# Fused hybrid-attention layer: q turned as unsplit pairs of heads, the windowed branch's output halves added on GpSimd, its row sums copied by VectorE

## The chip, the cores and the metric

The kernel runs on one core of one Trainium2 chip. A core has a matrix engine (TensorE, PE in the profile), VectorE (DVE), ScalarE (ACT), GpSimd (POOL) and a DMA-issuing engine (SyncE, SP). Each has its own instruction queue and works through it in order; the engines meet through semaphores. The metric is the time of one execution in microseconds, the median of several runs.

## What is computed

One layer of a diffusion backbone over 1024 latent tokens of width 1024 with 256 context tokens, batch 1, in float32. The tokens are modulated and projected; then two attentions run over the same tokens, each with 8 query heads of width 64 and 2 key heads (so four query heads share a key head):

```python
# windowed: |q_pos - k_pos| <= 128 and all 256 context keys, with a sink logit
scores = where(mask, q @ k.T / 8, -inf)
m = maximum(max(scores), sink); e = exp(scores - m)
p = e / (sum(e) + exp(sink - m));  o_a = p @ v
# global: all 1024 + 256 keys, q and k normalised
o_b = softmax(qn @ kn.T / 8) @ v
y = (g_a * (o_a @ w_branch_a) + g_b * (o_b @ w_branch_b)) @ w_out
```

A layer norm, a gated convolutional feed-forward block and a second layer norm follow. The change touches only the two attentions.

## The kernel before, in words

**Split numbers.** Products need more precision than one pass of the matrix engine gives, so a float32 operand is written as a rounded high part (type fp32r) and a remainder. The helper `split` (recorded at L84 and L87) does it in two instructions: a rounding copy and a subtraction.

**Units.** The attentions are cut into 32 units. A unit is one branch (0 windowed, 1 global), one tile `i` of 128 queries (0 to 7) and one key head `g` (0 or 1), with its four query heads; its name is branch_i_g, and in instruction names of the windowed branch this text writes i_g. Units 0 to 15 are windowed and take the stretch from about 330 to 455 us of the span, units 16 to 31 are global and end at about 722 us.

**Steps of a unit.** Each unit goes through these steps:

- `qprep`, two units ahead of its use: the 128x256 piece of q for four heads is split by GpSimd into `qs`, where each head has its 64 high and 64 low columns side by side. Four transposes on PE (L486) turn it, ScalarE copies the 128x512 result to `q1` (L489), with high parts on partitions 0 to 63 and low ones on 64 to 127, and two DMAs on SP's queue (L490, L491) write `q2` with the two halves exchanged. `qk` (L496, L497) multiplies keys with q1 and then q2, which gives all four products of high and low parts.
- `lat`, once for each head `h`: PE makes the scores (with the mask as one more matmul, L528, in the windowed branch), VectorE scales them into the tile `p` and takes the row's extreme (L545), ScalarE takes the exponential and the row sum (L547). In the windowed branch the row has one more column, the sink logit. GpSimd writes it for all four heads at once, ahead of head 0 (L542, `p<-sinkb`). A windowed row is 640 scores wide in the inner tiles, 641 with the sink.
- `norm` and `rows`: VectorE takes reciprocals of the row sums (L563), PE turns them (L567), in the windowed branch ScalarE copies the 4x128 result out of PSUM (L573), and SP writes it to DRAM (`dn`, L576) and reads it back spread over the partitions (`rb`, L578).
- value steps, one for each of 5 key tiles (10 in the global branch): four transposes of `p` on PE (L604), a split into `pth` (ScalarE, L615) and `ptl` (VectorE, L616), and two matmuls into `av` (L627, L628). For key tile 1 of a windowed unit (tiles 2 and 6 of a global one) the split is given to GpSimd: ScalarE copies the turned tile to the buffer `side` (L612), and GpSimd writes `pth` and `ptl` (L84, L87).
- `out_step`: ScalarE copies `av` to `side` (L639), GpSimd moves its lower half to `up` (L640), two adds of 64x256 make the output `ot` (L643), GpSimd multiplies it by `rb` (L646) and splits it into two parts `O` (L84, L87). The two adds run on VectorE for windowed tiles 0 to 5 (and in the very last unit), on GpSimd otherwise.

**What sets the order.** Scores of a unit and value steps of the unit before are interleaved by fixed fractions of a turn. In the windowed and global stages the instruction order on each engine comes out of a scheduler that works from that sequence, so an edit in one step can move others. The tile `p` has two buffers, so scores of the next unit are written while PE still turns the present one. `side` has two slots, used in turn.

Of the kernel before, what the change touches and what calls it, by code (L numbers as in the profile page):

```python
# [7 lines left out]
F32 = mybir.dt.float32  # L8
R32 = mybir.dt.float32r
AF = mybir.ActivationFunctionType  # L10
ALU = mybir.AluOpType
AX = mybir.AxisListType

P = 128
# [4 lines left out]
NT = 8  # L19
HD = 64  # L20
# [49 lines left out]
def layer_kernel(  # L70
# [6 lines left out]
    nc = tc.nc  # L77
    PSUM = bass.MemoryType.PSUM

    def split(src, hi, lo, hi_eng, lo_eng):  # L80
        if hi_eng is nc.scalar:
            nc.scalar.copy(hi, src)  # L82
        elif hi_eng is nc.gpsimd:
            nc.gpsimd.tensor_scalar(out=hi, in0=src, scalar1=1.0, scalar2=0.0, op0=ALU.mult, op1=ALU.add)  # L84
        else:
            hi_eng.tensor_copy(hi, src)
        lo_eng.tensor_tensor(out=lo, in0=src, in1=hi.bitcast(F32), op=ALU.subtract)  # L87
# [11 lines left out]
    ident = ctile([P, P], F32, "ident")  # L99
    identr = ctile([P, P], R32, "identr")  # L100
# [39 lines left out]
    qp = tc.alloc_tile_pool(name="qp", bufs=1, side="right", reuse_waits="tile")  # L140
# [144 lines left out]
    for k in range(KT):  # L285
# [9 lines left out]
        h, w = hT[k], w0[k]  # L295
# [84 lines left out]
    def qtile(br, t):  # L380
        return Q[br, t - t % 2][:, t % 2]
# [84 lines left out]
    class Unit:  # L466
# [11 lines left out]

        def qprep(self, mk=None):
            nm = self.id  # L480
            q3 = qtile(self.br, self.i)[:, self.g * 256:(self.g + 1) * 256].rearrange("p (h d) -> p h d", d=HD)
            qs = qp.tile([P, 4, P], R32, tag="qs", name=f"qs{nm}", bufs=2)
            split(q3, qs[:, :, 0:HD], qs[:, :, HD:P], nc.gpsimd, nc.gpsimd)
            tr = (mk or pt_tile)(f"qtr{nm}", R32)
            for h in range(4):
                nc.tensor.transpose(tr[:, h * P:(h + 1) * P], qs[:, h], identr)  # L486
            q1 = qp.tile([P, 512], R32, tag="q1", name=f"q1{nm}", bufs=2)
            q2 = qp.tile([P, 512], R32, tag="q2", name=f"q2{nm}", bufs=2)
            nc.scalar.copy(q1, tr)  # L489
            nc.sync.dma_start(q2[0:HD].bitcast(F32), q1[HD:P].bitcast(F32))  # L490
            nc.sync.dma_start(q2[HD:P].bitcast(F32), q1[0:HD].bitcast(F32))  # L491
            self.q = q1, q2

        def qk(self, o, h, ks, stop=True):
            hs = slice(h * P, (h + 1) * P)
            nc.tensor.matmul(o, self.q[0][:, hs], ks, start=True, stop=False)  # L496
            nc.tensor.matmul(o, self.q[1][:, hs], ks, start=False, stop=stop)  # L497
# [67 lines left out]
        def rows(self):  # L565
            tr = pt_tile(f"str{self.id}")
            nc.tensor.transpose(tr[0:4, 0:P], self.sm, ident)  # L567
            self.rb = att.tile([P, 2, P], F32, tag="rb", name=f"rb{self.id}", bufs=2)
            row = self.rb[0:4, 0]
            if self.br:  # L570
                nc.vector.reciprocal(row, tr[0:4, 0:P])
            else:
                nc.scalar.copy(row, tr[0:4, 0:P])  # L573
            dn = dpool.tile([4, P], F32, tag=f"dn{self.id}", name=f"dn{self.id}")
            tokens.append(f"dn{self.id}")
            nc.sync.dma_start(dn, row)  # L576
            for a in range(2):
                nc.sync.dma_start(self.rb[a * HD:(a + 1) * HD],  # L578
                                  dn.rearrange("(b a) q -> a b q", a=2)[a].partition_broadcast(HD))
# [15 lines left out]
        def value_steps(self):  # L595
            nm, kt = self.id, self.kt
# [33 lines left out]
            def out_step():  # L630
                av = self.av
                up = att.tile([HD, 512], F32, tag="up", name=f"up{nm}", bufs=1)
                ot = att.tile([P, 2, P], F32, tag="ot", name=f"ot{nm}", bufs=1)
                if last:
                    low = av
                    nc.scalar.copy(up, av[HD:P])
                else:
                    low = side_tile()
                    nc.scalar.copy(low, av)  # L639
                    nc.gpsimd.tensor_scalar(out=up, in0=low[HD:P], scalar1=1.0, scalar2=0.0, op0=ALU.mult, op1=ALU.add)  # L640
                oe = nc.gpsimd if (self.br or self.i >= NT - 2) and not last else nc.vector
                for h in range(2):
                    oe.tensor_tensor(out=ot[h * HD:(h + 1) * HD],  # L643
                                     in0=low[0:HD].rearrange("p (a b q) -> p a b q", b=2, q=P)[:, :, h],
                                     in1=up.rearrange("p (a b q) -> p a b q", b=2, q=P)[:, :, h], op=ALU.add)
                (nc.vector if last else nc.gpsimd).tensor_tensor(out=ot, in0=ot, in1=self.rb, op=ALU.mult)  # L646
                hf = self.i // 4
                qs = slice((self.i % 4) * P, (self.i % 4 + 1) * P)
                split(ot, otile(self.br, hf, 0, self.g)[:, :, qs], otile(self.br, hf, 1, self.g)[:, :, qs],
                      *((nc.scalar, nc.vector) if last else (nc.gpsimd, nc.gpsimd)))  # L650
# [1286 lines left out]
```

## Time and profile before

| | |
|---|---|
| median of 3 runs | 1526.8 us (1524.75, 1526.8, 1527.01) |
| profiled execution | 1523.1 us |
| its span | 1521.3 us |
| mean TensorE clock granted | 0.997 |
| windowed stage, about | 330 to 455 us |
| global stage, about | 455 to 722 us |

The profile gives the busy time of each engine (PEld is PE's weight load, which overlaps its matmuls), the instructions with start and duration, and for an idle time the instruction whose end released it. A timeline row reads: start in us, duration, engine, line, operation, tile written <- tiles read, shape and type, count, and in brackets the idle time ahead of it with its releaser. A group row reads: line, engine, operation, tiles, shape and count, then busy us and mean ns, then idle time. The ends of PE's instructions are modelled.

### The profile page before, as it was taken

The page shows a single profiled execution, that of the slowest core. Times are in us where ns is not written, and L with a number is a line of the kernel's source. Part 1 is how long each engine was busy: PE and PEld are TensorE (multiplying, and loading weights), DVE is VectorE, ACT ScalarE, POOL GpSimd, SP SyncE. Part 2 cuts the span into 40 slices and gives each one's busy share as a digit, 9 for nine tenths or more (in the row PEclk, how much of TensorE's full clock was granted, in tenths as well). Part 3 has the DMA queues.
Part 4 walks back from the last instruction along what each step waited for, and adds up shares of the span by engine and source line. Part 5 has one row for each costly group of instructions (what it writes and reads, how often), then busy time and mean ns, then how long its engine had stood idle before and what let it go on. Part 6 is the DMA issues. An engine that isn't in the chain of part 4 may idle for free.

```text
span 1521.3 us, 22183 instructions
## 1 busy us (share of the span) xinstructions
PE 1503.2 (99%) x7812; PEld 1263.3 (83%) x7812; DVE 1168.3 (77%) x1751; ACT 786.1 (52%) x1303; POOL 751.3 (49%) x727
## 2 busy tenths in 40 slices
PE   8999999999999999999999999999999999999997
PEld 7888888888988888887888998888888888888887
DVE  6667986539988787877865788888888888557884
ACT  5322222439988677667234555444444444435552
POOL 0356532426776677766124346666666773111121
PEclk9999999999999999999999999999999999999998
DMA  9777672322234576653541322333344448996731
GB/s 370 266 242 242 223 252 87 106 82 68 67 108 104 131 172 167 153 121 89 207 160 42 104 77 98 111 111 111 111 111 111 112 111 238 340 271 210 255 105 56
DMA packets 114399, 232.09 MB, mean 153 GB/s; under 512 B 13200, under 2 KB 28048, under 8 KB 114192
## 3 DMA queue, kind: packets, MB, share of 16 engines
q1 hardware_dynamic: 99056, 201.82, 39.8%
q0 software_dynamic: 10400, 20.19, 8.8%
q10 hardware_dynamic: 4832, 8.68, 1.5%
q8 instruction: 61, 1.00, 0.3%
q14 instruction: 50, 0.41, 0.1%
HBM read 179.45 MB, written 65.86 MB: 161 GB/s over the span
## 4 chain that ended last, share of the span: by engine, by line
PE 92%; DVE 3%; ACT 2%; issue 1%; DMA 1%; POOL 1%; SPq 0%; DVEq 0%; ACTq 0%; POOLq 0%
PE ptr L604 5%; PE p L90 4%; PE p L91 4%; PE p L92 4%; PE g L90 4%; PE g L92 4%; PE g L91 4%; PE av L627 4%; PE av L628 3%; PE b L90 3%; PE b L92 3%; PE b L91 3%; PE s L496 3%; PE s L497 3%; PE c L90 2%; PE c L92 2%
## 5 line engine op out<-in xcount | busy, mean ns | idle before, releaser
L616 DVE TENSOR_TENSOR ptl<-ptr,pth 128x512 fp32r<-128x512 f32 x195 | 128.2, 685 | 20.2 <-ACT pth L615 18.0
L547 ACT ACTIVATE p<-p,nm 128x1280 f32<-128x1280 f32 (+2 forms) x128 | 139.8, 1093 | 6.6 <-DVE p L545 5.9
L87 DVE TENSOR_TENSOR ld<-rd,hd 128x1024 fp32r<-128x1024 f32 x77 | 94.8, 1250 | 50.5 <-ACT hd L82 48.3
L615 ACT CAST pth<-ptr 128x512 fp32r<-128x512 f32 x195 | 111.3, 590 | 30.3 <-PE ptr L604 28.7
L82 ACT CAST hd<-rd 128x1024 fp32r<-128x1024 f32 x77 | 79.3, 1048 | 82.2 <-PE p L92 55.7
L604 PEld LDWEIGHTS ptr<-identr,pb 128*128 128x128 f32 x944 | 96.3, 140 | 23.7 <-ACT pb L550 3.0
L604 PE MATMUL ptr<-identr,pb 128*128 128x128 f32 x944 | 107.5, 245 | 1.5 <-ACT pb L550 1.0
L87 POOL TENSOR_TENSOR wlg<-wg,whg 128x512 fp32r<-128x512 f32 x32 | 48.6, 1529 | 121.7 <-ACT whg L82 80.8
L627 PE MATMUL av<-pth,VT 128*128 128x512 f32 x236 | 104.2, 441 | 0.5 <-ACT side L639 0.3
L90 PE MATMUL p<-hd 128*128 128x512 f32 x264 | 103.2, 391 | 0.0
L92 PE MATMUL p<-hd,ld 128*128 128x512 f32 x264 | 102.8, 389 | 0.0
L91 PE MATMUL p<-ld,hd 128*128 128x512 f32 x264 | 102.7, 389 | 0.0
L90 PE MATMUL g<-hh,whg 128*128 128x512 f32 x256 | 99.9, 390 | 0.0
L92 PE MATMUL g<-hh,wlg 128*128 128x512 f32 x256 | 99.7, 389 | 0.0
L91 PE MATMUL g<-hl,whg 128*128 128x512 f32 x256 | 99.6, 389 | 0.0
L628 PE MATMUL av<-ptl,VT 128*128 128x512 f32 x236 | 97.5, 413 | 0.3 <-DVE ptl L616 0.2
L545 DVE TENSOR_SCALAR_CACHE_REDUCE p<-s,cvt,nmc 128x1024 f32<-128x1024 f32 x64 | 84.2, 1317 | 5.2 <-PE s L497 5.2
L496 PE MATMUL s<-KL,q 128*128 128x512 f32 (+2 forms) x192 | 73.6, 384 | 1.3 <-DVE p L545 0.8
L497 PE MATMUL s<-KL,q 128*128 128x512 f32 (+2 forms) x192 | 71.8, 374 | 0.0
L783 ACT ACTIVATE sg<-g,bgc 128x512 f32<-128x512 f32 x32 | 22.0, 686 | 96.2 <-PE g L92 91.4
L82 ACT CAST wS<-s 128x512 fp32r<-128x512 f32 x76 | 45.3, 620 | 48.7 <-POOL s L1236 47.9
L82 ACT CAST wA<-ru 128x512 fp32r<-128x512 f32 x57 | 35.5, 623 | 62.6 <-PE d L92 33.6
(434 smaller groups left out, 4866.9 us busy)
## 6 DMA issues: line engine op xcount, KB each, us to landing
wml<-in_wmodT_dram SPq DMA_DIRECT2D x48, 512.0 KB
ru<-in_w_up_dram SPq DMA_DIRECT2D x38, 512.0 KB
rd<-td SPq DMA_DIRECT2D x55, 256.0 KB
rd<-sd SPq DMA_DIRECT2D x44, 256.0 KB
rd<-in_w_dn_dram SPq DMA_DIRECT2D x33, 256.0 KB
wm<-in_wmodT_dram SPq DMA_DIRECT2D x16, 512.0 KB
wg<-in_w_g_dram SPq DMA_DIRECT2D x32, 256.0 KB
sgd<-sg ACTq DMA_DIRECT2D x32, 256.0 KB
```

Of the source, the lines that this page charges most:

```text
L82: nc.scalar.copy(hi, src)
L87: lo_eng.tensor_tensor(out=lo, in0=src, in1=hi.bitcast(F32), op=ALU.subtract)
L90: nc.tensor.matmul(ps, a[0], b[0], start=start, stop=False, skip_group_check=resumed)
L91: nc.tensor.matmul(ps, a[0], b[1], start=False, stop=False, skip_group_check=resumed)
L92: nc.tensor.matmul(ps, a[1], b[0], start=False, stop=stop, skip_group_check=resumed)
L496: nc.tensor.matmul(o, self.q[0][:, hs], ks, start=True, stop=False)
L497: nc.tensor.matmul(o, self.q[1][:, hs], ks, start=False, stop=stop)
L547: nc.scalar.activation(row, row, AF.Exp, bias=self.nm[:, hs], scale=-1.0, accum_out=self.sm[:, hs])
L604: i = nc.tensor.transpose(tr[:, h * P:(h + 1) * P], self.bits[:, h, n * P:(n + 1) * P], identr)
L616: nc.vector.tensor_tensor(out=lo, in0=tr, in1=hi.bitcast(F32), op=ALU.subtract)
L627: nc.tensor.matmul(self.av, v, hi, start=first, stop=False)
L628: nc.tensor.matmul(self.av, v, lo, start=False, stop=self.left == 0)
```

## The change

Three edits, all in the attention units; the mask stays a matmul.

1. `qprep`: q is no longer split before it is turned. PE makes two float32 transposes, each of a pair of heads (128x128), into a 128x256 PSUM tile. ScalarE writes the rounded part `qx`, VectorE the remainder `qy` (both 128x256). Eight DMAs of 64x256 on SP's queue put each half of `qx` into both halves of q1's partitions and each half of `qy` into both of q2's, so q1 holds high parts twice and q2 low parts twice. `qk` picks the columns of a head accordingly.
2. `rows`: the windowed branch's 4x128 copy goes from ScalarE to VectorE.
3. `out_step`: the two adds run on GpSimd in every unit but the last.

```diff
@@ -478,20 +478,22 @@
 
         def qprep(self, mk=None):
             nm = self.id
-            q3 = qtile(self.br, self.i)[:, self.g * 256:(self.g + 1) * 256].rearrange("p (h d) -> p h d", d=HD)
-            qs = qp.tile([P, 4, P], R32, tag="qs", name=f"qs{nm}", bufs=2)
-            split(q3, qs[:, :, 0:HD], qs[:, :, HD:P], nc.gpsimd, nc.gpsimd)
-            tr = (mk or pt_tile)(f"qtr{nm}", R32)
-            for h in range(4):
-                nc.tensor.transpose(tr[:, h * P:(h + 1) * P], qs[:, h], identr)
-            q1 = qp.tile([P, 512], R32, tag="q1", name=f"q1{nm}", bufs=2)
-            q2 = qp.tile([P, 512], R32, tag="q2", name=f"q2{nm}", bufs=2)
-            nc.scalar.copy(q1, tr)
-            nc.sync.dma_start(q2[0:HD].bitcast(F32), q1[HD:P].bitcast(F32))
-            nc.sync.dma_start(q2[HD:P].bitcast(F32), q1[0:HD].bitcast(F32))
-            self.q = q1, q2
+            q2 = qtile(self.br, self.i)[:, self.g * 256:(self.g + 1) * 256]
+            tr = (mk or pt_tile)(f"qtr{nm}")[:, 0:2 * P]
+            for j in range(2):
+                nc.tensor.transpose(tr[:, j * P:(j + 1) * P], q2[:, j * P:(j + 1) * P], ident)
+            hi, lo = (qp.tile([P, 2 * P], R32, tag=f"q{a}", name=f"q{a}{nm}", bufs=2) for a in "xy")
+            nc.scalar.copy(hi, tr)
+            nc.vector.tensor_tensor(out=lo, in0=tr, in1=hi.bitcast(F32), op=ALU.subtract)
+            self.q = [qp.tile([P, 512], R32, tag=f"q{n}", name=f"q{n}{nm}", bufs=2) for n in (1, 2)]
+            for q, part in zip(self.q, (hi, lo)):
+                for a in range(2):
+                    for b in range(2):
+                        nc.sync.dma_start(q[b * HD:(b + 1) * HD, a * 256:(a + 1) * 256].bitcast(F32),
+                                          part[a * HD:(a + 1) * HD].bitcast(F32))
 
         def qk(self, o, h, ks, stop=True):
+            h = h % 2 * 2 + h // 2
             hs = slice(h * P, (h + 1) * P)
             nc.tensor.matmul(o, self.q[0][:, hs], ks, start=True, stop=False)
             nc.tensor.matmul(o, self.q[1][:, hs], ks, start=False, stop=stop)
@@ -570,7 +572,7 @@
             if self.br:
                 nc.vector.reciprocal(row, tr[0:4, 0:P])
             else:
-                nc.scalar.copy(row, tr[0:4, 0:P])
+                nc.vector.tensor_copy(row, tr[0:4, 0:P])
             dn = dpool.tile([4, P], F32, tag=f"dn{self.id}", name=f"dn{self.id}")
             tokens.append(f"dn{self.id}")
             nc.sync.dma_start(dn, row)
@@ -638,7 +640,7 @@
                     low = side_tile()
                     nc.scalar.copy(low, av)
                     nc.gpsimd.tensor_scalar(out=up, in0=low[HD:P], scalar1=1.0, scalar2=0.0, op0=ALU.mult, op1=ALU.add)
-                oe = nc.gpsimd if (self.br or self.i >= NT - 2) and not last else nc.vector
+                oe = nc.vector if last else nc.gpsimd
                 for h in range(2):
                     oe.tensor_tensor(out=ot[h * HD:(h + 1) * HD],
                                      in0=low[0:HD].rearrange("p (a b q) -> p a b q", b=2, q=P)[:, :, h],
```

Lines after the edit in `qprep` stand two higher than in the kernel before (L542 becomes L544, and so on).

The first place is GpSimd's queue in the middle of the windowed stage. In the names, `p_3_1<-sinkb` is the sink column of unit 3_1, and `pth`, `ptl`, `up`, `ot` carry their unit; the number at the end only tells tiles apart. Before:

```order
L542 TENSOR_SCALAR p_3_1_3822<-sinkb 128x4 [waits PE_49]
L646 TENSOR_TENSOR ot_2_0_3777<-ot_2_0_3777,rb_2_0_3621 128x256 [waits DMAHW6_49,DMAHW5_49,DVE_49]
L84 TENSOR_SCALAR O_3268<-ot_2_0_3777 128x2x128 [waits Pool_49]
L87 TENSOR_TENSOR O_3269<-ot_2_0_3777,O_3268 128x2x128 [waits Pool_49]
L84 TENSOR_SCALAR pth_3_0_1_3848<-side 128x512 [waits Activation_49]
L87 TENSOR_TENSOR ptl_3_0_1_3849<-side,pth_3_0_1_3848 128x512 [waits PE_49,Pool_49]
L84 TENSOR_SCALAR qs_5_1_4164<-Q_4_1588 128x4x64 [waits PE_49]
L640 TENSOR_SCALAR up_2_1_3902<-side 64x512 [waits Activation_49,Pool_49]
L87 TENSOR_TENSOR qs_5_1_4164<-Q_4_1588,qs_5_1_4164 128x4x64 [waits Pool_49]
L542 TENSOR_SCALAR p_4_0_3948<-sinkb 128x4 [waits PE_49]
```

and after:

```order
L544 TENSOR_SCALAR p_3_0_3728<-sinkb 128x4 [waits PE_49]
L84 TENSOR_SCALAR pth_2_1_1_3754<-side 128x512 [waits DVE_49,Activation_49]
L87 TENSOR_TENSOR ptl_2_1_1_3755<-side,pth_2_1_1_3754 128x512 [waits PE_49,Pool_49]
L642 TENSOR_SCALAR up_2_0_3808<-side 64x512 [waits Activation_49,Pool_49]
L645 TENSOR_TENSOR ot_2_0_3809<-side,up_2_0_3808 64x256 [waits Pool_49]
L645 TENSOR_TENSOR ot_2_0_3809<-side,up_2_0_3808 64x256
L648 TENSOR_TENSOR ot_2_0_3809<-ot_2_0_3809,rb_2_0_3649 128x256 [waits DMAHW2_49,DMAHW1_49,Pool_49]
L84 TENSOR_SCALAR O_3284<-ot_2_0_3809 128x2x128 [waits Pool_49]
L87 TENSOR_TENSOR O_3285<-ot_2_0_3809,O_3284 128x2x128 [waits Pool_49]
L544 TENSOR_SCALAR p_3_1_3858<-sinkb 128x4 [waits PE_49]
```

Between two sink columns there stood the product and `O` of one unit, then `pth`, `ptl`, `up` and q's split; the column came ahead of the product. Now the whole output of unit 2_0, its two halves included, stands between `up` and the column of unit 3_1, and the column comes last.

The second place is ScalarE's queue at the same units: the exponentials that wait for GpSimd are head 0 of units 3_0 and 3_1. Before:

```order
L547 ACTIVATE p_3_0_3696,sm_3_0_3695<-p_3_0_3696,nm_3_0_3694 128x641 [waits DVE_49,Pool_49]
L612 COPY side<-ptr_2_1_1_3717 128x512 [waits PE_49]
L573 COPY rb_2_1_3747<-str_2_1_3745 4x128 [waits DMAHW1_49,DMAHW0_49,DMAHW7_49,PE_49,Pool_49]
L615 CAST pth_2_1_2_3768<-ptr_2_1_2_3763 128x512 [waits DVE_49,PE_49]
L547 ACTIVATE p_3_0_3696,sm_3_0_3695<-p_3_0_3696,nm_3_0_3694 128x641 [waits DVE_49]
L639 COPY side<-av_2_0_3682 128x512 [waits PE_49]
L547 ACTIVATE p_3_0_3696,sm_3_0_3695<-p_3_0_3696,nm_3_0_3694 128x641 [waits DVE_49]
```

and after:

```order
L549 ACTIVATE p_3_0_3728,sm_3_0_3727<-p_3_0_3728,nm_3_0_3726 128x641 [waits DVE_49,Pool_49]
L617 CAST pth_2_1_0_3734<-ptr_2_1_0_3729 128x512 [waits PE_49]
L614 COPY side<-ptr_2_1_1_3749 128x512 [waits PE_49]
L617 CAST pth_2_1_2_3800<-ptr_2_1_2_3795 128x512 [waits DVE_49,PE_49]
L641 COPY side<-av_2_0_3714 128x512 [waits PE_49]
L549 ACTIVATE p_3_0_3728,sm_3_0_3727<-p_3_0_3728,nm_3_0_3726 128x641 [waits DVE_49] x3
L486 CAST qx_4_0_3821<-qtr_4_0_3818 128x256 [waits DMAHW6_49,DMAHW3_49,DMAHW7_49,DMAHW2_49,PE_49]
L552 CAST pb_3_0_3793<-onec 128x1 [waits Activation_49]
L617 CAST pth_2_1_3_3840<-ptr_2_1_3_3835 128x512 [waits PE_49]
L617 CAST pth_2_1_4_3852<-ptr_2_1_4_3847 128x512 [waits PE_49]
L549 ACTIVATE p_3_1_3858,sm_3_1_3857<-p_3_1_3858,nm_3_1_3856 128x641 [waits DVE_49,Pool_49]
```

In both, head 0 of a unit stands ahead of the copy `side<-ptr` of the unit before it, for which GpSimd's `pth` waits. The `pth` cast that stood ahead of the exponential now stands between it and that copy, the row copy `rb<-str` is gone, and `qx` has half the width.

The third place is SP's queue there, with `dn` and `rb` of unit 2_0 or 2_1 and the q copies of later units. Before:

```order
L578 DMA rb_2_0_3621<-dn_2_0_3623 64x2x128 [waits DMAHW5_49,DMAHW6_49,DMAHW4_49,Pool_49]
L578 DMA rb_2_0_3621<-dn_2_0_3623 64x2x128
L490 DMA q_3_1_3669<-q_3_1_3668 64x512 [waits Activation_49]
L491 DMA q_3_1_3669<-q_3_1_3668 64x512 [waits DMAHW0_49]
L576 DMA dn_2_1_3749<-rb_2_1_3747 4x128 [waits DMAHW1_49,Activation_49]
L578 DMA rb_2_1_3747<-dn_2_1_3749 64x2x128 [waits DMAHW2_49,DMAHW1_49,Pool_49]
L578 DMA rb_2_1_3747<-dn_2_1_3749 64x2x128 [waits DMAHW3_49]
```

and after:

```order
L580 DMA rb_2_0_3649<-dn_2_0_3651 64x2x128 [waits DMAHW5_49,DMAHW1_49,Pool_49]
L580 DMA rb_2_0_3649<-dn_2_0_3651 64x2x128 [waits DMAHW2_49]
L492 DMA q_3_1_3695<-qx_3_1_3691 64x256 [waits DMAHW3_49]
L492 DMA q_3_1_3695<-qx_3_1_3691 64x256 [waits DMAHW4_49]
L492 DMA q_3_1_3696<-qy_3_1_3692 64x256 [waits DVE_49,PE_49]
L492 DMA q_3_1_3696<-qy_3_1_3692 64x256 [waits DMAHW6_49]
L492 DMA q_3_1_3696<-qy_3_1_3692 64x256 [waits DMAHW7_49]
L492 DMA q_3_1_3696<-qy_3_1_3692 64x256 [waits DMAHW0_49]
L578 DMA dn_2_1_3781<-rb_2_1_3779 4x128 [waits DMAHW1_49,DVE_49]
L492 DMA q_4_0_3825<-qx_4_0_3821 64x256 [waits DMAHW2_49,PE_49,Activation_49]
L580 DMA rb_2_1_3779<-dn_2_1_3781 64x2x128 [waits DMAHW3_49,DMAHW1_49,Pool_49]
L580 DMA rb_2_1_3779<-dn_2_1_3781 64x2x128 [waits DMAHW4_49]
```

Two q copies a unit have become eight, some of them wait for VectorE's `qy`, and they stand in between a unit's `dn` and its `rb`.

## The prediction

> **What bounds the kernel now.** I read the page first, for what is busy, then the busy time by stretch, then the timelines of the windowed stage.
>
> ```profile
> PE 1503.2 (99%) x7812; PEld 1263.3 (83%) x7812; DVE 1168.3 (77%) x1751; ACT 786.1 (52%) x1303; POOL 751.3 (49%) x727
> ```
>
> PE is busy nearly throughout, but its ends are modelled, so the two attention stages need a closer look. By stretch (busy us of PE, PEld, DVE, ACT, POOL; then clock, DMA share, GB/s):
>
> ```profile
> 360.00:440.00 80.00, 79.43 (x567) 70.95 (x566) 73.79 (x157) 73.86 (x175) 62.52 (x94) 1.00 0.29 75
> 470.00:720.00 250.00, 249.10 (x1526) 204.21 (x1524) 200.80 (x387) 179.04 (x313) 173.94 (x218) 1.00 0.60 140
> ```
>
> In the global stage (470 to 720) PE has 0.9 us idle in 250 while DVE, ACT and POOL have 49 to 76 us to spare: only PE counts there. In the windowed stage (360 to 440) PE, DVE and ACT are all above 92%, and POOL has 17.5 us idle. There a queue that waits can lengthen the turn. One turn of POOL's queue, from one unit's pooled part to the next:
>
> ```profile
> 401.61 0.62 POOL L84 TENSOR_SCALAR pth<-side 128x512 fp32r<-128x512 f32 x1 [0.76 <-PE str L567]
> 402.31 1.29 POOL L87 TENSOR_TENSOR ptl<-side,pth 128x512 fp32r<-128x512 f32 x1
> 403.99 0.41 POOL L84 TENSOR_SCALAR qs<-Q 128x256 fp32r<-128x256 f32 x1 [0.38 <-PE qtr L486]
> 404.47 0.62 POOL L640 TENSOR_SCALAR up<-side 64x512 f32<-64x512 f32 x1
> 405.18 0.97 POOL L87 TENSOR_TENSOR qs<-Q,qs 128x256 fp32r<-128x256 f32 x1
> 406.12 0.37 POOL L542 TENSOR_SCALAR p<-sinkb 128x4 f32<-128x4 f32 x1
> 406.51 0.75 POOL L646 TENSOR_TENSOR ot<-ot,rb 128x256 f32<-128x256 f32 x1
> 407.35 0.40 POOL L84 TENSOR_SCALAR O<-ot 128x256 fp32r<-128x256 f32 x1
> 407.84 0.74 POOL L87 TENSOR_TENSOR O<-ot,O 128x256 fp32r<-128x256 f32 x1
> ```
>
> The row to watch is the sink column (L542), 0.37 us. The first exponential of a unit reads that column, so it cannot start before POOL has written it. The same write at other units gives the turn's length:
>
> ```profile
> 361.28 0.20 POOL L542 TENSOR_SCALAR p<-sinkb 128x4 f32<-128x4 f32 x1
> 367.01 0.38 POOL L542 TENSOR_SCALAR p<-sinkb 128x4 f32<-128x4 f32 x1
> 436.91 0.37 POOL L542 TENSOR_SCALAR p<-sinkb 128x4 f32<-128x4 f32 x1
> 447.15 0.21 POOL L542 TENSOR_SCALAR p<-sinkb 128x4 f32<-128x4 f32 x1
> ```
>
> The second and third belong to units 2_1 and 7_0, nine turns apart: (436.91 - 367.01) / 9 = 7.77 us a turn.
>
> **The output halves, and the place of the sink column.** On VectorE a half takes 416 ns alone; on GpSimd, where the global units already do it, 734 ns:
>
> ```profile
> L643 POOL TENSOR_TENSOR ot<-side,up x38: 721/734/742, 442.6 to 713.1; 64x256 f32<-64x256 f32 x38
> L643 DVE TENSOR_TENSOR ot<-side,up x24: 416/590/1486, 349.9 to 436.3; 64x256 f32<-64x256 f32 x24
> 405.13 1.30 DVE L643 TENSOR_TENSOR ot<-side,up 64x256 f32<-64x256 f32 x2 [0.60 <-POOL up L640]
> ```
>
> VectorE loses 1.30 + 0.60 = 1.9 us a turn, its wait for `up` included. The q split leaves POOL (0.41 + 0.97) and two halves come (about 1.5), so POOL's load hardly changes. What changes is the order. In POOL's new queue the sink column of unit n+1 stands behind the pooled `pth` and `ptl` of unit n-1 and the whole output of n-2: `up`, two halves, product with `rb`, both parts of `O`; before, it stood ahead of the last three. On ScalarE the first exponential of unit n stands ahead of the copy `side<-ptr` of n-1, which feeds that `pth`. This closes a ring: sink column, exponential, side copy, the whole POOL chain, next sink column. Its length is one turn at the least.
>
> The POOL part, with a unit of the windowed end where GpSimd already does the halves, and the only steady write that follows an `O`:
>
> ```profile
> 441.88 0.61 POOL L640 TENSOR_SCALAR up<-side 64x512 f32<-64x512 f32 x1 [2.53 <-ACT side L639]
> 442.58 1.53 POOL L643 TENSOR_TENSOR ot<-side,up 64x256 f32<-64x256 f32 x2
> 444.19 0.73 POOL L646 TENSOR_TENSOR ot<-ot,rb 128x256 f32<-128x256 f32 x1
> 360.58 0.73 POOL L87 TENSOR_TENSOR O<-ot,O 128x256 fp32r<-128x256 f32 x1
> ```
>
> From start to start: `pth` 0.70, `ptl` 1.29 (its row), `up` 0.70, two halves 1.61, product 0.84, `O` 0.49, its remainder 0.70 (360.58 to 361.28), sink column 0.20. Sum 6.53 us. The ScalarE part:
>
> ```profile
> 361.51 0.84 ACT L547 ACTIVATE p<-p,nm 128x641 f32<-128x641 f32 x1 [0.46 <-DVE ptl L616]
> 362.35 0.56 ACT L612 COPY side<-ptr 128x512 f32<-128x512 f32 x1
> 406.04 0.59 ACT L615 CAST pth<-ptr 128x512 fp32r<-128x512 f32 x1
> 406.51 0.21 ACT L550 CAST pb<-onec 128x1 fp32r<-128x1 f32 x1
> 400.95 0.58 ACT L612 COPY side<-ptr 128x512 f32<-128x512 f32 x1
> ```
>
> The exponential at 361.51 starts 0.03 after the column's end at 361.48, after 0.46 idle; the profile names VectorE, but the column is what came last, so this wait exists already where `O` stands ahead. Then 0.84 to the next instruction, 0.47 for the `pth` cast that stands between (406.04 to 406.51), 0.58 for the copy and 0.08 until POOL starts (401.53 to 401.61): 2.00 us. The ring is 6.53 + 2.00 = 8.53 us against 7.77. Bounds: bare durations without gaps give about 8.05; a column of 0.37, as in most rows, gives 8.70. I take 8.53, since the gaps are measured. Nine turns: 9 x 0.76 = +6.8 us (2.5 to 8.4).
>
> The Trainium skill, GPSIMD Engine Reference, section "4.1 Engine selection", speaks against this edit: elementwise work with two inputs belongs on VectorE, GpSimd being about twice as slow. The rows give 734 / 416 = 1.76, so the direction agrees and the size is smaller; at twice 416 the ring would be 0.2 us longer and the sum 1.8 us higher (an estimate from that page).
>
> The ramp and the tail of the stage: the turn from 361.28 to 367.01 takes 5.73 us now and would take the ring's 8.53, +2.8, but the write at 361.28 itself stands earlier in the new order, ahead of the product and `O`, which can give it all back: +1.5 (0 to 2.8). The last turn, 436.91 to 447.15, is 10.24 us now; at 8.53 it gives back 1.7: -1.5 (-1.7 to 0).
>
> **The row copy.** ScalarE loses sixteen copies, VectorE gains them.
>
> ```profile
> L573 ACT COPY rb<-str x16: 238/254/256, 344.9 to 456.4; 4x128 f32<-4x128 f32 x16
> ```
>
> On VectorE no such row exists; the nearest is its 128x4 reciprocal, 0.18, below, so 0.2 a turn. VectorE has 1.9 us freed and ScalarE idles inside the ring: nothing on the path (-0.25 to +0.25 a turn if neither cover held, which the ring excludes).
>
> ```profile
> 406.46 0.18 DVE L563 RECIPROCAL sm<-sm 128x4 f32<-128x4 f32 x1
> ```
>
> **The q turn.** On PE four fp32r transposes become two fp32 ones of the same size:
>
> ```profile
> 573.07 0.46 PE L486 MATMUL qtr<-identr,qs 128*128 128x128 f32 x4
> 573.36 0.33 PE L604 MATMUL ptr<-identr,pb 128*128 128x128 f32 x2
> 1483.28 0.42 PE L1758 MATMUL zt<-ident,pr 128*128 128x128 f32 x2
> 1483.54 0.28 PE L1761 MATMUL stl<-onec,pr 128*128 128x1 f32 x2
> ```
>
> Four took 0.29 to the next start, two fp32 ones 0.26: PE is even (at most 0.03 x 32 = -1 us). ScalarE's cast halves, from 0.58 to some 0.35 (between 0.25 and 0.58); VectorE gains a 128x256 subtraction, between the 0.2 of the reciprocal and the 0.69 of `ptl`, say 0.4. Both lie beside PE in the global stage (49 us of VectorE spare for 15 units' 6 us) and inside the ring in the windowed one. With that cover gone they would cost 0.4 x 10 = 4 us. The q DMAs:
>
> ```profile
> 405.36 0.50 SPq L490 DMA_DIRECT2D q<-q  x1
> 405.90 0.60 SPq L491 DMA_DIRECT2D q<-q  x1
> 403.11 1.29 SPq L578 DMA_DIRECT2D rb<-dn  x2
> 401.90 0.26 SPq L576 DMA_DIRECT2D dn<-rb  x1
> ```
>
> Two become eight, 8 x 0.55 = 4.4 us of SP's queue where 1.1 stood; with the 1.29 and 0.26 it holds 5.95 us of a turn of 8.5. Behind the waiting q copies stand `dn` and `rb`, for which POOL's product waits, and the loads of the stage. q is made two units ahead, so I cost this at nothing; the bound is rival C.
>
> The Trainium skill, DMA: Bandwidth & Descriptors, section "Measured (HBM→SBUF, 128 partitions, SWDGE, issued from GpSimd)", says that transfers should be batched and that those under 64 KB are dominated by their descriptors; eight quarter pieces go against that. It bears on rival C; no run here shows transfers of this size on that queue, and the sum goes by the issue rows.
>
> Global stage: 0 (-0.5 to +1), since PE alone counts. Sum: 6.8 + 1.5 - 1.5 + 0 = +6.8 us (0.3 to 12.2). The profiled execution took 1523.1 us and would take 1529.9; it lies 3.7 us under the median of the runs, so on the median of 1526.8 the forecast is **1533.6 us**, by itself 1527 to 1539.
>
> **The rivals.** *A, relief:* if the ring is shorter than I read (the column early enough), the freed VectorE and ScalarE time shortens the turn until PE binds. For it: PE's value matmuls are slower here than over the program,
>
> ```profile
> L627 PE MATMUL av<-pth,VT 128*128 128x512 f32 x51 | 23.4, 460 | 0.3 <-ACT side L639 0.3
> L627 PE MATMUL av<-pth,VT 128*128 128x512 f32 x236 | 104.2, 441 | 0.5 <-ACT side L639 0.3
> ```
>
> so the turn could fall by 441/460 to 7.45: 10 x -0.32 = -3.2, and -1 at the tail, -4.2: 1522.6 us. Against it: the ring's rows. It decides for itself only if the ring is under 7.45. *B, no change:* the ring is there but comes out at about 7.7, hidden by the present turn: 1526 us. It needs POOL's chain 0.8 us shorter than its rows. *C, the q copies bind:* if each of the eight issues or its landing takes about 0.9 us instead of 0.55, SP's queue is full for 8 x 0.9 + 1.55 = 8.75 us a turn, POOL's product waits for `rb` inside the ring, and a turn goes to about 9: ten turns x 0.5 = +5 more, 1539 us.
>
> **How the numbers follow.** Forecast 0.63, A 0.13, B 0.12, C 0.12. The range 1524 to 1540 leaves out about half of A and a third of C. What a measurement can tell from no change is 0.2%, 3.05 us. Faster (under 1523.7): 0.10 of A and 0.01 of B, 0.11. Same: 0.03 of A, 0.09 of B, 0.06 of the forecast's low end, 0.18. Slower: 0.57 of the forecast, C and 0.02 of B, 0.71.
>
> **What would show it.** Right: sink columns 8.3 to 8.7 us apart between units 2_1 and 7_0; ScalarE idle ahead of the first exponential, which starts within 0.1 us of the column's end; POOL's wait ahead of `pth` (0.76 us above) released by the side copy; PE under 95% busy from 360 to 440. The global stage keeps its length within 1 us. Wrong: columns 7.4 to 7.8 us apart (A or B); or POOL's product idle for `rb`, or PE's first score matmul for q (C).

## The result, and the profile after

The changed kernel takes 1535.62 us (median of 6 runs, 1534.33 to 1537.28) against 1525.55 us for the kernel before (6 runs, 1524.66 to 1527.01). The ratio is 1.0065, 95% interval 1.0052 to 1.0078: slower by some 10 us. The prediction was 1533.6 us, or 6.8 us more than before. The profiled execution of the changed kernel took 1537.28 us, with a span of 1535.5 us, and lies 1.7 us above its median; that of before lies 2.5 us under its own. So the two profiles are 14.2 us apart, and what follows shares out those 14.2 us. In the experiments below, one run of the halves alone took 1646.13 us at a granted clock of 0.85 and is left out of its median.

The page's busy times, and the two stretches that the prediction began with:

```profile
PE 1504.7 (98%) x7748; PEld 1261.2 (82%) x7748; DVE 1172.2 (76%) x1775; ACT 777.9 (51%) x1287; POOL 729.0 (47%) x687
```

```profile
360.00:440.00 80.00, 73.58 (x493) 63.11 (x492) 59.61 (x136) 61.90 (x146) 56.10 (x85) 0.98 0.38 90
470.00:720.00 250.00, 249.22 (x1514) 205.07 (x1513) 210.09 (x418) 181.23 (x320) 167.39 (x203) 1.00 0.66 156
```

In the windowed stage PE falls from 79.4 to 73.6 us busy in 80, and no other engine takes over: all of them are busy less. The global stage looks as before. GpSimd's queue over one turn of the windowed stage:

```profile
380.91 0.20 POOL L544 TENSOR_SCALAR p<-sinkb 128x4 f32<-128x4 f32 x1
383.11 0.62 POOL L84 TENSOR_SCALAR pth<-side 128x512 fp32r<-128x512 f32 x1 [1.99 <-ACT side L614]
383.81 1.29 POOL L87 TENSOR_TENSOR ptl<-side,pth 128x512 fp32r<-128x512 f32 x1
385.18 0.62 POOL L642 TENSOR_SCALAR up<-side 64x512 f32<-64x512 f32 x1
385.88 1.52 POOL L645 TENSOR_TENSOR ot<-side,up 64x256 f32<-64x256 f32 x2
387.49 0.74 POOL L648 TENSOR_TENSOR ot<-ot,rb 128x256 f32<-128x256 f32 x1
388.31 0.40 POOL L84 TENSOR_SCALAR O<-ot 128x256 fp32r<-128x256 f32 x1
388.80 0.73 POOL L87 TENSOR_TENSOR O<-ot,O 128x256 fp32r<-128x256 f32 x1
389.50 0.20 POOL L544 TENSOR_SCALAR p<-sinkb 128x4 f32<-128x4 f32 x1
```

and ScalarE's rows that stand between the two columns:

```profile
381.15 0.83 ACT L549 ACTIVATE p<-p,nm 128x641 f32<-128x641 f32 x1 [1.21 <-POOL p L544]
381.98 0.56 ACT L617 CAST pth<-ptr 128x512 fp32r<-128x512 f32 x1
382.44 0.58 ACT L614 COPY side<-ptr 128x512 f32<-128x512 f32 x1
389.73 0.83 ACT L549 ACTIVATE p<-p,nm 128x641 f32<-128x641 f32 x1 [1.20 <-POOL p L544]
```

This is the ring, link by link: column, 0.04 us, exponential, cast, side copy, 0.09 us, GpSimd's whole chain, next column, 389.50 - 380.91 = 8.59 us later. ScalarE idles 1.2 us a turn for a column that takes 0.20. In the list of waits from 360 to 440 (total us, times, longest) it is among the largest, and PE's own largest wait is for the side copy, which stands in the ring behind that exponential:

```profile
ACT p L549 <- POOL p L544: 9.6, 8, 1.2
PE ptr L606 <- ACT side L614: 5.9, 8, 0.8
```

Where the 14.2 us lie is read from four marks that both traces have (us from the span's start; the last column is the stretch since the mark above):

| mark | before | after | stretch longer by |
|---|---|---|---|
| sink column of unit 2_1 | 367.01 | 372.80 | 5.8 |
| sink column of unit 7_0, nine turns on | 436.91 | 449.68 | 7.0 |
| first score matmul `sx` of the global stage | 451.6 | 465.3 | 0.9 |
| last two adds of `ot` (VectorE) | 721.4 | 734.4 | -0.7 |
| end of the span | 1521.3 | 1535.5 | 1.2 |

By these marks the nine turns take 8.54 us each, where 8.53 was predicted, and the ramp ahead of them lost 5.8 us where 1.5 was predicted. But the column does not stand at the same place of a unit's work in both orders: before, it is ahead of GpSimd's product, after, behind it. A mark that stays is the last of a unit's four exponentials, here of 2_1 and 7_0, before and after:

```profile
374.06 0.83 ACT L547 ACTIVATE p<-p,nm 128x641 f32<-128x641 f32 x1
443.38 0.73 ACT L547 ACTIVATE p<-p,nm 128x513 f32<-128x513 f32 x1
```

```profile
377.71 0.82 ACT L549 ACTIVATE p<-p,nm 128x641 f32<-128x641 f32 x1
455.08 0.71 ACT L549 ACTIVATE p<-p,nm 128x513 f32<-128x513 f32 x1
```

By this mark the ramp lost 3.65 us, the nine turns 8.05 (8.60 us a turn against 7.70), and the stretch to the first `sx` 2.0. In the ramp the waits are others than in the ring. VectorE's row copy, then PE's next rows and GpSimd's product in the ramp:

```profile
357.42 0.28 DVE L575 COPY rb<-str 4x128 f32<-4x128 f32 x1 [1.70 <-POOL ot L648]
```

```profile
357.75 0.53 PE L606 MATMUL ptr<-identr,pb 128*128 128x128 f32 x4 [1.50 <-DVE rb L575]
359.32 0.44 PE L499 MATMUL s<-KL,q 128*128 128x384 f32 x1 [1.03 <-DMA q<-qy]
```

```profile
363.55 0.74 POOL L648 TENSOR_TENSOR ot<-ot,rb 128x256 f32<-128x256 f32 x1 [1.15 <-DMA rb<-dn]
```

VectorE stood for 1.70 us behind a buffer `rb` that GpSimd's product still held, PE waited for VectorE, and then for q's copies; the product then waited for `rb`. Right behind PE's waits its granted clock (third number from the end) is lower:

```profile
355.00:360.00 5.00, 2.47 (x19) 2.08 (x18) 2.58 (x7) 4.36 (x13) 4.57 (x7) 0.96 0.43 98
360.00:365.00 5.00, 5.00 (x29) 4.43 (x28) 2.42 (x5) 2.25 (x5) 2.28 (x5) 0.69 0.32 78
```

In the trace of before the same ten microseconds ran at 1.00. The missing 0.04 and 0.31 of five microseconds each come to some 1.7 us of TensorE's time (an estimate from these two rows), which is part of the ramp's loss.

### The profile page after: what moved, and what is told of

It is laid out like the page before. It is cut to its first block, busy times and chain, and to the rows that moved or that the text cites. A ratio compares the mean times of both kernels' runs of the same rounds, so it can differ in the third digit from the quotient of the medians.

```text
span 1535.5 us, 22451 instructions
## 1 busy us (share of the span) xinstructions
PE 1504.7 (98%) x7748; PEld 1261.2 (82%) x7748; DVE 1172.2 (76%) x1775; ACT 777.9 (51%) x1287; POOL 729.0 (47%) x687
## 4 chain that ended last, share of the span: by engine, by line
PE 87%; POOL 4%; DVE 3%; issue 2%; DMA 1%; ACT 1%; SPq 1%; DVEq 0%; POOLq 0%; ACTq 0%
PE p L90 4%; PE p L92 4%; PE p L91 4%; PE g L90 4%; PE g L92 4%; PE g L91 4%; PE ptr L606 3%; PE b L90 3%; PE b L92 3%; PE b L91 3%; PE av L629 3%; PE av L630 3%; PE c L90 2%; PE c L91 2%; PE d L91 2%
## 5 line engine op out<-in xcount | busy, mean ns | idle before, releaser
L606 PEld LDWEIGHTS ptr<-identr,pb 128*128 128x128 f32 x944 | 99.4, 141 | 34.4 <-ACT side L614 10.4
```

The lines of the kernel that those rows point to most:

```text
L606: i = nc.tensor.transpose(tr[:, h * P:(h + 1) * P], self.bits[:, h, n * P:(n + 1) * P], identr)
```

## The experiments

The rows below name a turn twice: the time from the sink column of 2_1 to that of 7_0, divided by nine, which is the turn that the recorded expectations speak of, and the same between the last exponentials of these units, which keep their place. Each median stands beside the kernel before measured with it.

| kernel | median us | before us | difference | turn us, by column | by last exponential |
|---|---|---|---|---|---|
| the kernel before | 1525.55 | | | 7.77 | 7.70 |
| the change | 1535.62 | 1525.55 | +10.1 | 8.54 | 8.60 |
| change, column on VectorE | 1531.99 | 1524.69 | +7.3 | 8.40 | 8.31 |
| halves alone | 1525.85 | 1524.69 | +1.2 | 8.10, 7.69 without the first | 7.79 |
| q turn and row copy | 1531.44 | 1524.69 | +6.8 | 8.04 | 8.08 |
| q turn alone | 1530.21 | 1524.69 | +5.5 | 8.17 | 8.23 |
| change, four q copies | 1533.09 | 1524.53 | +8.6 | 8.60 | 8.62 |
| q turn alone, four copies | 1530.47 | 1524.53 | +5.9 | 8.32 | 8.23 |
| before, eight q copies | 1534.42 | 1524.53 | +9.9 | 7.67 | 8.22, of which one of 11.33 |
| change, row copies back | 1529.62 | 1524.53 | +5.1 | 8.49 | 8.24 |
| change, four copies, column on VectorE | 1530.71 | 1524.88 | +5.8 | 8.24 | 8.22 |
| the same, row copies back | 1530.66 | 1524.88 | +5.8 | 8.36 | 8.27 |
| halves, column on VectorE, q as before | 1523.37 | 1524.88 | -1.5 | 7.71 | 7.72 |
| before, one more reader of the turned q | 1527.56 | 1524.66 | +2.9 | 8.04 | 8.00 |

**The ring opened.** The changed kernel, with

```diff
-                    nc.gpsimd.tensor_scalar(out=self.p[:, :, n], in0=sinkb[...
+                    nc.vector.tensor_scalar(out=self.p[:, :, n], in0=sinkb[...
```

> The changed kernel with one edit: the sink column is written by VectorE instead of GpSimd. Ring theory: the first exponential no longer waits for GpSimd's chain, so a turn of the windowed stage falls from 8.54 us to 7.4 to 7.8, nine turns give back 7 to 10 us, and the time comes to 1525 to 1529 us, the rest being the ramp. Rival, that the halves cost by GpSimd's own load or by the q copies on SP's queue: the turn stays over 8.3 us and the time at 1534 to 1537 us.

1531.99 us (ratio to before 1.0051, 1.0038 to 1.0063). The time lies between the two theories, the turn is the rival's: the loss falls from 10.1 to 7.3 us, so 2.8 come back, but the turn falls only to 8.40 (8.31 by the exponentials). ScalarE no longer waits for a column, and PE's weight loads wait elsewhere, as the list of waits from 328 to 470 shows:

```profile
PEld s L499 <- DMA q<-qy: 6.8, 8, 1.2
```

**One edit at a time.** The third edit alone:

```diff
-                oe = nc.gpsimd if (self.br or self.i >= NT - 2) and not last else nc.vector
+                oe = nc.vector if last else nc.gpsimd
```

> The kernel before with the third edit alone: the output halves on GpSimd. Here the sink column stands behind the q split and the two halves of a unit but ahead of its product and O. Ring theory: 0.70 + 1.38 for pth and ptl, 0.49 + 0.70 + 0.75 for the q split and up, 1.61 for the halves, 0.20 for the column and 2.0 on ScalarE make 7.8 us, so a turn of 7.8 to 8.0 and 1525 to 1529 us. Rival, that the halves on GpSimd cost by themselves: a turn near 8.5 us and 1531 to 1535 us.

1525.85 us (1.0007, 0.9998 to 1.0016): the halves alone cost next to nothing. After one long first turn of 11.4 us the turn is 7.69; the column keeps its place ahead of the product. The expectation's sum gave 7.8 as the least, so it was 0.1 us too long. The changed kernel without the third edit:

> The changed kernel with the third edit undone: the halves of windowed tiles 0 to 5 on VectorE again. Here the sink column stands right behind up, ahead of product and O. Ring theory: the ring is about 0.70 + 1.38 + 0.70 + 0.20 + 2.0 = 5.0 us and does not bind; a turn is 7.4 to 7.8 us; only the ramp's cost stays, so 1526 to 1531 us. Rival, that eight q copies bind: the turn is over 8.3 us and the time 1533 us or more.

1531.44 us (1.0049, 1.0035 to 1.0063). The time came a little above the range, the turn at 8.04 above what the ring theory allowed. No ring is there, and PE waits for q throughout (waits from 328 to 470):

```profile
PEld s L499 <- DMA q<-qy: 10.0, 10, 1.3
```

The first edit alone, with the halves and the row copy as before:

> The kernel before with the first edit alone: q turned as unsplit pairs, eight q copies. If the ramp's loss comes from the q copies on SP's queue, it stays: 1527 to 1531 us, with PE waiting for q copies between 345 and 372 us. If it comes from VectorE's row copy waiting for the buffer rb, it goes: 1523 to 1526 us.

1530.21 us (1.0041, 1.0028 to 1.0053). The time is that of the first theory, the place is not: PE waits for q copies from 375 us on, not before. More than half of the whole loss comes with the q turn alone, the edit that the prediction costed at nothing. By the column's marks: ramp +1.2, nine turns +3.6, the stretch to the first `sx` +2.5, global stage -2.2 (in its profiled run, which took 1528.24 us, the lowest of its five).

**The number of copies.** In the changed kernel ScalarE and VectorE write two quarters of q1 and q2 in place, so four copies are left:

```diff
-            for q, part in zip(self.q, (hi, lo)):
-                for a in range(2):
-                    for b in range(2):
-                        nc.sync.dma_start(q[b * HD:(b + 1) * HD, ...], part[a * HD:(a + 1) * HD]...)
+            hi, lo = ([q[a * HD:(a + 1) * HD, a * 256:(a + 1) * 256] for a in range(2)] for q in self.q)
...
+                for a in range(2):
+                    nc.sync.dma_start(q[(1 - a) * HD:(2 - a) * HD, a * 256:(a + 1) * 256]..., part[a]...)
```

> The changed kernel with four q copies instead of eight: ScalarE and VectorE write two quarters of q1 and q2 where they belong, and only the other two are copied. The sink column still stands last in GpSimd's queue. Ring theory: the turn stays at 8.5 to 8.6 us; only the ramp and the end of the stage, where PE waits for q copies, get better: 1529 to 1533 us. Rival, that the q copies set the turn: it falls under 8.2 us and the time under 1529 us.

1533.09 us (1.0056, 1.0044 to 1.0069). As the ring theory had it, but for 0.1 us of the time: the ramp got 3.5 us shorter (column of 2_1 at 369.27 instead of 372.80), the turn stayed at 8.60, and the wait for the column stayed too (375 to 440):

```profile
ACT p L550 <- POOL p L545: 5.6, 8, 0.7
```

The same four copies without the other two edits:

> The kernel before with the first edit alone and four q copies instead of eight; the halves and the row copy are where they were. If the loss of the first edit (1530 us with eight copies) comes from the number of copies on SP's queue: PE no longer waits for q copies, the turn is 7.4 to 7.8 us against 8.17, and the time 1522 to 1526 us. Rival, that the loss comes from the subtraction on VectorE or from the chain through two engines: 1528 us or more.

1530.47 us (1.0036, 1.0023 to 1.0048): the rival. PE's waits for copies are gone from the turns, and the turn is 8.32 by the column, 8.23 by the exponentials as with eight copies. Fewer copies took PE's wait for q away, and no time with it. In the list of waits from 375 to 440 PE has one wait left, once in each of eight turns, for a cast of `pth` on ScalarE:

```profile
PE av L630 <- ACT pth L618: 4.0, 8, 0.5
```

The same list of the kernel before has no wait of PE. The kernel before with its two copies cut into eight:

```diff
-            nc.sync.dma_start(q2[0:HD].bitcast(F32), q1[HD:P].bitcast(F32))
-            nc.sync.dma_start(q2[HD:P].bitcast(F32), q1[0:HD].bitcast(F32))
+            for c in range(0, 512, P):
+                nc.sync.dma_start(q2[0:HD, c:c + P].bitcast(F32), q1[HD:P, c:c + P].bitcast(F32))
+                nc.sync.dma_start(q2[HD:P, c:c + P].bitcast(F32), q1[0:HD, c:c + P].bitcast(F32))
```

> The kernel before, with each of its two q copies cut into four (eight copies of 64x128, the bytes unchanged). If the number of copies on SP's queue is what costs: a turn of 7.9 to 8.3 us, PE waiting for q copies, 1527 to 1531 us. If it is the first edit's other work: no change, 1523 to 1526 us.

1534.42 us (1.0063, 1.0049 to 1.0077), more than either theory said, but with a turn of 7.67: eight copies cost 9.9 us and hardly touch the steady turn. They cost at both ends of the stage and behind it. The column of 2_1 comes 5.5 us later than before (372.46; the next turn gives 1.4 of it back), the stretch from 7_0 to the first `sx` is 4.0 us longer (18.7 against 14.7), and the global stage 4.4 us (274.2 against 269.8), whose cause stays open. A lower clock of TensorE goes with it: the granted clock of the five runs is 0.993 to 0.995, where the kernel before had 0.996 to 0.998, and in the profile it falls to 0.81 and 0.85 in the two stretches of 5 us from 360 and to 0.66 in that from 445. In the ramp (350 to 375) the product waits for `rb`, queued behind q's copies on SP:

```profile
POOL ot L647 <- DMA rb<-dn: 6.0, 2, 4.1
```

and at the other end (441 to 475) PE waits for q itself:

```profile
PE s L498 <- DMA q<-q: 2.7, 2, 2.2
```

**The row copy back on ScalarE.** The changed kernel with `nc.scalar.copy(row, ...)` again:

> The changed kernel with the second edit undone: row copies on ScalarE again. In its order GpSimd writes the sink column ahead of the product and O again, behind the halves. Ring theory: 0.70 + 1.38 + 0.70 + 1.61 + 0.20 + 2.0 = 6.6 us, so the ring does not bind; what is left is the q copies with a turn of 8.0 to 8.3 us, 1529 to 1532 us. Rival, that eight copies and the halves together give 8.5 us whatever the place of the column: 1534 us or more.

1529.62 us (1.0030, 1.0021 to 1.0039): the loss is 5.1 us instead of 10.1. The time is within the ring theory's range. The turn by the column is not, 8.49, which is what the rival said; but here the columns come 5.4 to 10.6 us apart, and by the last exponentials the turn is 8.24, within the range. By that mark the gain is shared: 3.0 us ahead of unit 2_1 and 3.2 in the nine turns. PE now waits for q in some of the turns (375 to 440):

```profile
PE s L499 <- DMA q<-qy: 3.0, 6, 1.2
```

One such wait is shown by the chain that ended last, from an exponential of one unit to the score matmul of a later one (start, duration, what; pieces of 0.14 us and less left out):

```profile
400.58 0.93 ACT p L549 x2
401.52 0.42 SPq L492
401.99 0.59 SPq L492
402.63 0.59 SPq L492
403.26 0.59 SPq L492
403.95 0.54 SPq L492
404.54 0.60 SPq L492
405.18 0.59 SPq L492
405.81 2.00 DMA q<-qy
407.95 0.61 PE s L499
```

Seven issues in a row take 4.3 us, the last copy another 2.0 to land, and PE waits for it.

**Both bounds taken away.** Four copies and the column on VectorE:

> The changed kernel with both suspected bounds taken away: the sink column written by VectorE and four q copies instead of eight. If the ring and the q copies are the two bounds, one close behind the other, only both together give the turn back: 7.4 to 7.9 us, 1524 to 1528 us. Rival, a third bound in the first edit itself, its two more instructions on ScalarE and VectorE between the exponentials (the first edit with four copies had a turn of 8.37 us with no wait for copies): the turn stays over 8.2 us and the time at 1529 to 1532 us.

1530.71 us (1.0038, 1.0026 to 1.0051), a turn of 8.24: the rival. Opening the ring shortens the turn by 0.4 us (8.60 with four copies and the column on GpSimd), and a third bound stands behind the other two. PE's wait is again the one for `pth` (375 to 440):

```profile
PE av L630 <- ACT pth L618: 3.5, 8, 0.4
```

With the row copies on ScalarE as well:

> As the kernel with four copies and the column on VectorE, but with the row copies on ScalarE again. If the row copy's engine matters (with the ring and eight copies its return gave 6 us, all of it ahead of unit 2_1): 1 us or more faster than the version with it on VectorE. If what it gave came only from the other order of GpSimd's queue: the same within 1 us, or slower by ScalarE's 0.25 us a turn.

1530.66 us (1.0037, 1.0024 to 1.0049), the same. So here, with neither ring nor eight copies, the row copy's engine does not matter. This speaks for the 5.0 us that its return gave having come with the other order of the queues, where GpSimd's column stands ahead of the product again; that order was not tried by itself.

**The halves without the q turn.** The kernel before with the third edit and the column on VectorE:

> The kernel before with the third edit (halves on GpSimd) and the sink column on VectorE; q is split and turned as before. Ring theory: without the column GpSimd's queue gates nothing and VectorE has 1.9 us a turn to spare, so the turn is at most the 7.69 us of the halves alone, and the time 1522 to 1526 us. Rival, that the halves on GpSimd or a column on VectorE cost by themselves: 1528 us or more.

1523.37 us (0.9991, 0.9982 to 1.0000), a turn of 7.71. As the ring theory had it. It is the fastest kernel of all, by 1.5 us over the one before, within what can be told from no change.

**The third bound.** In the version with four copies and nothing else, one unit's q is handled like this, first on ScalarE, then on VectorE:

```profile
407.65 0.75 ACT L488 CAST q<-qtr 64x256 fp32r<-64x256 f32 x2
```

```profile
408.43 0.87 DVE L490 TENSOR_TENSOR q<-qtr,q 64x256 fp32r<-64x256 f32 x2 [0.31 <-ACT q L488]
```

PE's transposes ran at 405.3, so the PSUM buffer of the turned q, one of three, was taken for 4.0 us, against 1.9 before, and VectorE stood 0.31 us for ScalarE. To try a longer hold without copies and with hardly any work:

```diff
             nc.scalar.copy(q1, tr)
+            qd = qp.tile([P, 1], F32, tag="qd", name=f"qd{nm}", bufs=2)
+            nc.vector.tensor_tensor(out=qd, in0=tr[:, 0:1].bitcast(F32), in1=q1[:, 0:1].bitcast(F32), op=ALU.subtract)
```

> The kernel before with one small instruction more for each unit: after ScalarE's cast of the turned q, VectorE subtracts one column (128x1) of it into a scratch tile. No copy is added and hardly any work; what it adds is that the PSUM buffer of the turned q, one of three that the turned p and q share, is given back only when VectorE has come to it, as in the first edit (4.0 us from the transposes to the last reader with four copies, against 2.0 before). If this hold is the third bound: a turn of 8.0 us or more and 1527 to 1531 us. Rival, that it is the first edit's work or the order that the scheduler makes of it: a turn of 7.7 to 7.8 us and 1524 to 1526 us.

1527.56 us (1.0016, 1.0006 to 1.0025), a turn of 8.04. Both fall within what the hold theory said, from an instruction of 0.16 us. But the turns are uneven: 8.3 to 8.5 us from 385 to 410 us, 7.8 after. In a long turn, the transposes of q on PE and VectorE's last reading of their result:

```profile
390.56 0.46 PE L486 MATMUL qtr<-identr,qs 128*128 128x128 f32 x4
394.83 0.15 DVE L491 TENSOR_TENSOR qd<-qtr,q 128x1 f32<-128x1 f32 x1
```

and in the first of the short ones, with ScalarE's cast between them:

```profile
407.37 0.47 PE L486 MATMUL qtr<-identr,qs 128*128 128x128 f32 x4
408.69 0.58 ACT L489 CAST q<-qtr 128x512 fp32r<-128x512 f32 x1
410.40 0.16 DVE L491 TENSOR_TENSOR qd<-qtr,q 128x1 f32<-128x1 f32 x1
```

The buffer was held for 4.4 us in the one and 3.2 in the other, and 3.2 also in the four units that follow. A hold of 3.2 us instead of 1.9 thus cost some 0.07 us a turn (7.77 against 7.70), and the average of 8.04 comes mostly from three long turns. In their stretch PE waits 0.6 us once for VectorE's instruction. Nor does the hold set the order of the other versions: the one with four copies and the column on VectorE holds the buffer for 5.2 us at a turn of 8.24, the one with four copies alone for 4.0 at 8.32. Whether the long turns come from the longer hold or from the other order that the scheduler makes around the instruction is not told apart. Some of the 2.9 us is again the clock: the three runs at 0.998 took 1526.15 to 1526.57 us, under the hold theory's range, the one at 0.994 1529.87. The third bound stays open; what the traces show is PE waiting for ScalarE's cast of `pth` in each turn.

## Why the prediction was right in time and only half right in cause

**The ring.** Predicted 8.53 us a turn and +6.8 over nine turns; by the same columns measured 8.54 and +7.0. The links stand as predicted, but the agreement to 0.01 is partly luck. The steady turns take 8.58 to 8.61 us: `ptl` takes 1.37 us from start to start, where its bare row of 1.29 was put in. The 8.54 contains one turn of 8.11, and the 7.77 of before contains turns of 8.12 and 7.88, where the steady one is 7.70. By the last exponentials nine turns cost 8.05 us. That the ring binds is shown by two versions: with the column still last and PE's waits for q gone the turn stayed at 8.60, and the same version with the column on VectorE turned in 8.24.

**The step that failed** is "q is made two units ahead, so I cost this at nothing". The q turn alone costs 5.5 us, more than half of the loss, and makes the turn 8.17 without any ring. By the last exponentials every version with the q turn and without the ring turns in 8.1 to 8.3 us, with eight copies or four, and every version with the halves and without the q turn in 7.7 to 7.8. Opening the ring gave back only 2.8 us of 10.1, because this bound stands 0.3 to 0.4 us a turn behind it (8.22 to 8.31 against 8.60). In the changed kernel the ring hides the q turn in the steady turns, as the prediction said; it left out that the q turn's bound stays when the ring is opened, and that at both ends of the stage there is no such cover.

**Rival C had one of the mechanisms, with the wrong condition.** It was to decide from 0.9 us an issue, when SP's queue is full. The issues took about 0.64 us from start to start, and q was late all the same. Both of C's signs stand in the ramp: PE's score matmul waited 1.03 us for q, GpSimd's product 1.15 us for `rb`. What counts there is the chain: cast, eight issues one after the other, 2.0 us to land, score matmuls. But it is not the whole price of the q turn: with four copies PE's waits for q are gone from the turns and the loss is 5.9 us. The prediction said that no run shows transfers of this size on that queue; the `rb` reads are 64 KB each, the size of the new q copies, and go through it in the kernel before.

**Ramp, tail, global stage.** By the columns, ramp: predicted +1.5, at most +2.8; measured +5.8. The prediction took the 5.73 us from 361.28 to 367.01 for a turn, but the first of these columns stands behind an `O` and the second ahead of one; the last exponentials of these units are 7.4 us apart. Part of the 5.8 is that change of place (3.65 by the exponentials), the rest the waits for q and for `rb` and the lower clock behind them, which the ring's sum does not contain. Eight copies in the kernel before cost 5.5 us there, four in place of eight gave 3.5 back. Tail: predicted -1.5, measured +0.9 (+2.0 by the exponentials), and 2.5 us with the q turn alone, whose late copies PE also waits for there. Global stage: predicted 0, measured -0.7, and -2.2 with the q turn alone. That its two transposes in place of four account for it was not tried.

**The row copy** was costed at nothing. In the ramp of the changed kernel it stood 1.7 us for `rb` and PE behind it, but with the ring open and four copies its engine made no difference (1530.66 and 1530.71). That it counts through the order of the queues fits this and was not shown by itself.

**Rivals A and B** needed a shorter ring and are out.

**Luck.** The time came within 2.0 us of the forecast, the difference within 3.3 (10.1 against 6.8), since the kernel before came out at 1525.55 us and not at 1526.8. Between the two profiles the forecast missed 7.4 of 14.2 us. The whole rise was put down to the halves, which alone cost 1.2 us. The edits taken one by one (q turn and row copy 6.8, halves 1.2) come to 8.0, where all together cost 10.1; of the versions measured, only those with all three edits have the ring.

## What to carry to other kernels

Where one queue's write gates another engine, walk the ring through both queues in the new order and add it up: that sum came within 0.07 us of the steady turn. Then look for the bound next behind it before pricing what the ring hides, and price the stage's ends, where no ring is turning yet, by themselves. Measure turns and ends by a mark that keeps its place in both orders. A row of DMA issues is a latency, not only a load: count how many stand in a row between the producer and its reader, and add the landing. But taking a wait away is not yet a gain: with four copies the wait was gone and the time was not.

## What the runs showed of the hardware that was not expected

VectorE's two adds of `ot` take 658 ns each in the kernel before and 413 ns in the version with q turn and row copy, where the same adds meet no q split on GpSimd (groups of VectorE from 375 to 440):

```profile
L643 DVE TENSOR_TENSOR ot<-side,up 64x256 f32<-64x256 f32 x17 | 11.2, 658 | 4.9 <-POOL up L640 4.7
```

```profile
L645 DVE TENSOR_TENSOR ot<-side,up 64x256 f32<-64x256 f32 x16 | 6.6, 413 | 0.1
```

The Trainium skill, GPSIMD Engine Reference, section "8. Key points", says that GpSimd shares its SBUF interfaces with VectorE and that VectorE's instructions with two SBUF inputs contend for them; the trace agrees, with a factor of 1.6 for these adds. GpSimd's column, 0.37 us in most of its rows before, right behind the q split, takes 0.20 in every row after. The split is not the reason by itself: the version with the q turn and four copies has no split, and there the column takes 0.45 us beside VectorE's adds. Whether the adds are the reason was not tried.

The granted clock falls for 5 to 15 us at a time and not in every version. In the trace of before no stretch of 5 us from 325 to 480 is under 1.00; in that of the change one is at 0.69, with one more reader of the turned q one is at 0.50. Over the six runs of the change it goes with the time: 1534.33 us at a mean clock of 0.998, 1537.28 at 0.994. What makes it fall was not tried.
